# Seven block products in place of eight in nine of 22 tile pairs of an MLP, and its output product in three groups of rows

## The chip, the cores and the metric

The kernel runs on one core of a Trainium2 chip. The metric is the device time of one execution in microseconds (us). The engines are called PE (TensorE, the matmuls; PEld is its weight loads), DVE (VectorE), ACT (ScalarE), POOL (GpSimd) and SP (SyncE, which issues the DMAs). Each engine takes its instructions from a queue of its own, in order.

## The reference

A network on 16 + 512 positions of 1024 features: a layer with differential attention, a layer with latent attention, and a mixer with a convolution and sliding attention. Each ends in a gated MLP of the same kind with 2816 = 22 x 128 hidden features, and the change is in these three MLPs alone:

```python
xn = rms_norm(h, g_norm)
a, b = jnp.split(xn @ w_in, 2, axis=-1)
ap = jnp.pad(a, ((0, 0), (CONV_W - 1, 0), (0, 0)))
a_conv = conv_b
for j in range(CONV_W):
    a_conv = a_conv + ap[:, j:j + L] * conv_w[j]
return h + (jax.nn.silu(a_conv) * b) @ w_out
```

The first MLP has 528 positions, the second 514 on the a side and 512 on the b side, the third 512.

## The kernel before

Features lie on partitions, positions along the free axis. h, the residual stream, stays in SBUF in float32. Each heavy product keeps the precision of float32 with reduced-precision operands: a tensor is split into a high part (a cast) and a low part (the rest), and `lin` (L243) issues three matmuls for each tile of 128 input features: high x high, high x low, low x high. All of them are line 254.

Weights come through the class `Weights` (L73) by one plan, a list of chunks of 8 x 128 rows in the order of use. `load` issues the DMA (L86, 512 KB) three chunks ahead, `_split` makes the parts two chunks ahead: ACT casts the high part (L103), and DVE takes the low part in two halves of 512 columns (L112), or, for every fourth chunk, POOL in four pieces of 256 (L108).

`ffn` (L411) is an MLP. For each of the 22 tiles f of 128 hidden features it makes two products over all 1024 input features, a (`pa`) and b (`pb`). a is multiplied by the norm's factor R on DVE (L434, `am`); the gate follows: the first tap of the convolution on ACT (L437), two more on DVE (L441), silu on ACT (L444), times R (L445), times b (L448); and the result is split into Gh and Gl (L351, L352). R comes late: its sum of squares ends after the last residual add, so the first tile's matmuls run before R is there, and its `am` waits. In the first MLP both products run in two ranges of columns (a in 272 and 258, b in 272 and 256), in the second a in 258 and 256 and b in one of 512, in the third each in one of 512. Once all 22 tiles of G stand, `proj_h` (L398), or `finish` (L1252) in the last MLP, makes the output product: for each of 8 tiles m of output features, 22 tiles of G in three chunks of weights into one accumulation in PSUM, which is then added into h.

The order on each engine is set by a scheduler that works from the order of the code, and waits between engines are semaphores.

## Time and profile before

| | |
|---|---|
| median of 3 runs | 2115.77 us (2115.68 to 2116.41) |
| the profiled execution | 2117.24 us, of which the span of its instructions is 2115.5 |
| PE busy | 2083.4 us, 98% of the span |
| PEld busy | 1868.7 us, 88% |
| DVE busy | 1163.7 us, 55% |
| ACT busy | 858.1 us, 41% |
| POOL busy | 447.4 us, 21% |
| granted TensorE clock | 0.994 of full speed |

A busy share is an average over the span. An engine is busy while one of its instructions runs. Matmuls are pipelined, so the duration of one is longer than the distance from its start to the next one's; a rate of PE is read from starts.

### The profile page before, as it was taken

The numbers are of one execution on the slowest core, as the hardware profiler recorded it, in microseconds if no ns is written. First come the engines' busy times: TensorE is split into PE (matmuls) and PEld (weight loads), VectorE is DVE, ScalarE is ACT, GpSimd is POOL, SyncE is SP. The second block draws the span as 40 slices with busy tenths as digits, with TensorE's granted clock in tenths as the row PEclk, the third lists the DMA queues.
The fourth block names the chain that finished last, engine by engine and source line by source line (L and its number), as shares of the span: only waits on it lengthen the run. The fifth ranks groups of instructions, "written<-read, shape, count | busy, mean of one in ns | idle before, by whom it ended". The sixth has DMA issues, their size and how long they took to land.

```text
span 2115.5 us, 33036 instructions
## 1 busy us (share of the span) xinstructions
PE 2083.4 (98%) x13226; PEld 1868.7 (88%) x13226; DVE 1163.7 (55%) x2212; ACT 858.1 (41%) x1658; POOL 447.4 (21%) x555
## 2 busy tenths in 40 slices
PE   8999999999999999999999999999999999999998
PEld 8999899999999988899999888788888888888887
DVE  8687756666533477755555532675534355555322
ACT  6566544444323455543333332354422334333221
POOL 5223231111121231122111123221112231111121
PEclk9999999999999999999999999999999999999999
DMA  4111022222322211122322333222223232333331
GB/s 168 51 60 60 32 81 100 81 90 90 93 83 88 77 36 35 41 70 81 100 91 91 94 90 105 85 90 71 75 75 100 91 98 90 100 100 96 88 98 58
DMA packets 52954, 174.72 MB, mean 83 GB/s; under 512 B 6080, under 2 KB 9024, under 8 KB 52800
## 3 DMA queue, kind: packets, MB, share of 16 engines
q1 hardware_dynamic: 52368, 172.34, 25.7%
q8 instruction: 104, 1.70, 0.3%
q14 instruction: 50, 0.41, 0.1%
q10 hardware_dynamic: 432, 0.27, 0.1%
HBM read 170.45 MB, written 2.10 MB: 82 GB/s over the span
## 4 chain that ended last, share of the span: by engine, by line
PE 92%; DVE 5%; ACT 2%; issue 1%; POOL 0%; DMA 0%; POOLq 0%; DVEq 0%; ACTq 0%
PE po L254 24%; PE pa L254 18%; PE pb L254 18%; PE pc L254 6%; PE pq L254 5%; PE pg L254 4%; PE s L482 2%; PE pyc L254 2%; PE pd L254 2%; PE pm L254 2%; PE ph L254 1%; PE o L1122 1%; PE pya L254 1%; PE pt L1100 1%; DVE wlo L112 1%
## 5 line engine op out<-in xcount | busy, mean ns | idle before, releaser
L103 ACT CAST whi<-raw 128x1024 fp32r<-128x1024 f32 (+3 forms) x328 | 330.8, 1009 | 723.9 <-PE po L254 233.1
L108 POOL TENSOR_TENSOR wlo<-raw,whi 128x256 fp32r<-128x256 f32 (+1 forms) x342 | 264.3, 803 | 1089.8 <-ACT whi L103 1085.1
L112 DVE TENSOR_TENSOR wlo<-raw,whi 128x512 fp32r<-128x512 f32 (+2 forms) x474 | 318.7, 714 | 220.7 <-ACT whi L103 218.8
L254 PE MATMUL pa<-Xh,wlo 128*128 128x258 f32 (+3 forms) x880 | 269.3, 306 | 0.0
L254 PE MATMUL pa<-Xl,whi 128*128 128x258 f32 (+3 forms) x880 | 269.0, 306 | 0.0
L254 PE MATMUL pa<-Xh,whi 128*128 128x258 f32 (+3 forms) x880 | 268.3, 305 | 0.0
L254 PE MATMUL po<-Gl,whi 128*128 128x512 f32 (+2 forms) x726 | 244.1, 336 | 0.0
L254 PE MATMUL po<-Gh,whi 128*128 128x512 f32 (+2 forms) x726 | 242.8, 334 | 0.0
L254 PE MATMUL po<-Gh,wlo 128*128 128x512 f32 (+2 forms) x726 | 242.5, 334 | 0.0
L254 PE MATMUL pb<-Xh,wlo 128*128 128x512 f32 (+2 forms) x704 | 238.9, 339 | 0.0
L254 PE MATMUL pb<-Xl,whi 128*128 128x512 f32 (+2 forms) x704 | 238.7, 339 | 0.0
L254 PE MATMUL pb<-Xh,whi 128*128 128x512 f32 (+2 forms) x704 | 238.1, 338 | 0.0
L254 PEld LDWEIGHTS pa<-Xl,whi 128*128 128x128 f32 x880 | 165.6, 188 | 8.6
L254 PEld LDWEIGHTS pa<-Xh,whi 128*128 128x128 f32 x880 | 165.8, 188 | 8.2
L254 PEld LDWEIGHTS pa<-Xh,wlo 128*128 128x128 f32 x880 | 166.1, 189 | 6.6
L254 PEld LDWEIGHTS po<-Gh,whi 128*128 128x128 f32 x726 | 136.6, 188 | 16.2
L254 PEld LDWEIGHTS po<-Gh,wlo 128*128 128x128 f32 x726 | 136.4, 188 | 14.8
L254 PEld LDWEIGHTS po<-Gl,whi 128*128 128x128 f32 x726 | 136.7, 188 | 14.3
L254 PEld LDWEIGHTS pb<-Xh,wlo 128*128 128x128 f32 x704 | 132.6, 188 | 14.5
L254 PEld LDWEIGHTS pb<-Xh,whi 128*128 128x128 f32 x704 | 132.4, 188 | 14.2
L254 PEld LDWEIGHTS pb<-Xl,whi 128*128 128x128 f32 x704 | 132.4, 188 | 14.1
L434 DVE TENSOR_TENSOR am<-pa,R 128x272 f32<-128x272 f32 (+2 forms) x110 | 52.9, 481 | 141.9 <-PE pa L254 133.8
(394 smaller groups left out, 4468.9 us busy)
## 6 DMA issues: line engine op xcount, KB each, us to landing
raw<-in_w_in_dram SPq DMA_DIRECT2D x134, 512.0 KB, 3.4
raw<-in_w_up_dram SPq DMA_DIRECT2D x44, 512.0 KB, 3.4
raw<-in_w_out_dram SPq DMA_DIRECT2D x32, 512.0 KB, 3.5
raw<-in_w_qkv_dram SPq DMA_DIRECT2D x24, 512.0 KB, 3.5
raw<-in_w_o_dram SPq DMA_DIRECT2D x16, 512.0 KB, 3.4
raw<-in_w_dn_dram SPq DMA_DIRECT2D x16, 512.0 KB, 3.5
raw<-in_w_out_dram SPq DMA_DIRECT2D x16, 384.0 KB, 3.1
raw<-in_w_co_dram SPq DMA_DIRECT2D x8, 512.0 KB, 3.4
```

The lines of the kernel that those rows point to most:

```text
L103: nc.scalar.copy(h, r)
L108: nc.gpsimd.tensor_tensor(l[:, c], r[:, c], h[:, c].bitcast(F32), op=ALU.subtract)
L112: nc.vector.tensor_tensor(l[:, c], r[:, c], h[:, c].bitcast(F32), op=ALU.subtract)
L254: nc.tensor.matmul(ps, w, x, start=first and i == 0, stop=last and i == len(ops) - 1)
L434: nc.vector.tensor_tensor(am[:, sa - a0 : ea - a0], pa[:, : ea - sa], R[:, sa:ea], op=ALU.mult)
L482: nc.tensor.matmul(s[:, :w], qa[:, q0 : q0 + P], ka[:, k0:k1], start=z == 0, stop=z == len(ops) - 1 and not masked,)
L1100: nc.tensor.transpose(t[:, b * P : (b + 1) * P], p[:, j, a : a + P], self.ident)
L1122: nc.tensor.matmul(o[:, i, j, :], st[n, "pt", j][:, b * P : (b + 1) * P], V[:, b, c], start=n % 4 == j == b == 0, stop=False,)
```

## The change

The 22 tiles are put in three groups (`GROUPS`): 8, 7 and 7 tiles. Nine times two tiles (f, g) form a pair; tiles 0, 1, 14 and 21 stay plain. In a pair, g is done as before. The tile f takes its a rows and b rows together: a and b are two rows of blocks, the input features two columns (the tiles 0 to 3 and 4 to 7), the positions two halves, and a product of 2 x 2 by 2 x 2 blocks that takes 8 block products is done by 7, with sums of weights and of inputs. A block product is 12 matmuls (four tiles of features, three matmuls each) on half of the positions: 264 columns in the first MLP, 258 in the second, 256 in the third.

The sums of inputs, four for each of four tiles of features, are T0 to T3. `differences` makes them once in each MLP, after tile 0 in the code: for each k, ACT scales h into x, DVE forms four tensors in one buffer d, ACT casts all four at once into Th, DVE takes the low part Tl. The sums of weights are made by POOL for each pair: S (two sums, in four pieces of 256 columns), t (two sums, four pieces) and the low part of d (two pieces). S and the d of `differences` have the same tag, "rawS", with one buffer. A pair loads two rows at once, the second into a buffer "rawA" of its own kind. The number of bytes loaded stays.

Within a pair PE's order is written out by hand. With X for the input and the weights in front: A (a rows, X), C (S, T0), half of g's a product, A += (S, T1), B (a rows, X), the rest of g's a product, A += (t, T2), half of g's b product, C += (t, X), A += (d, T3), the rest of g's b product. Between these, ACT copies A to p1, C to bm, A to u2 and A to bm, and DVE adds the pieces into `an` and `bm`. The gate works on all positions at once. Where the third MLP has one range, g's a product stands whole between C and A += (S, T1).

After each of the first two groups its output product, over 8 or 7 tiles of G, is added into h; the last group's goes on as the whole did before. In the first MLP the ranges are 264 and 264.

```diff
+GROUPS = (
+    (0, 8, (0, 1, (2, 3), (4, 5), (6, 7))),
+    (8, 15, ((8, 9), (10, 11), (12, 13), 14)),
+    (15, 22, ((15, 16), (17, 18), (19, 20), 21)),
+)
...
+    def sums(self, d, a, b, op):
+        for c in (slice(0, 256), slice(256, 512)):
+            self.net.nc.gpsimd.tensor_tensor(d[:, c], a[:, c], b[:, c], op=op)
...
+        if kind == "s":
+            self.S = self.more.tile([P, 1056], F32, tag="rawS", name=f"rawS{n}", bufs=1)
+            self.sums(self.S[:, lo], a2[:, lo], a2[:, hi], ALU.add)
+            self.sums(self.S[:, hi], self.S[:, lo], a1[:, lo], ALU.subtract)
+            return self.S[:, :1024]
+        if kind == "t":
+            self.sums(a1[:, lo], a1[:, lo], a2[:, lo], ALU.subtract)
+            self.sums(a1[:, hi], a1[:, hi], self.S[:, hi], ALU.subtract)
+            return a1
+        return a2[:, hi]
...
+                f, g = st
+                rows = [self.chunk(wi, m)[1][0] for m in (f, NF + f)]
+                pl += [((wi, f, "a"), rows, 8, P, "a"), ((wi, f, "s"), [], 8, P, "s"), self.chunk(wi, g)]
+                pl += [((wi, f, "t"), [], 8, P, "t"), self.chunk(wi, NF + g), ((wi, f, "d"), [], 4, P, "d")]
+            pl += [self.chunk(wo, m, k0, k1) for m in range(KD)]
...
+    def group_h(self, psp, name, G, k0, nk, ranges, done):
+        for m in range(KD):
+            w = [(self.W.get((name, m, k0)), 0)]
+            ps = [psp.tile([P, 512], F32, tag="mm", name=self.n("po")) for _ in ranges]
+            for a, b in ((0, nk),) if m else ((0, nk - 2), (nk - 2, nk)):
+                for p, (s, e) in zip(ps, ranges):
+                    self.lin(p[:, : e - s], w, G, s, e, part=(a, b), first=a == 0, last=b == nk)
+            for p, (s, e) in zip(ps, ranges):
+                done(p[:, : e - s], m, s, e)
...
+            def differences():
+                for k in range(4):
+                    g = self.pc(xg, k + 4)
+                    x = tp.tile([P, NT], F32, tag="am", name=self.n("x"))
+                    nc.scalar.activation(x[:, : NT - s0], self.h[:, k, s0:], AF.Identity, scale=self.pc(xg, k))
+                    x1, x2 = x[:, :H], x[:, s1 - s0 : e1 - s0]
+                    d = tp.tile([P, 1056], F32, tag="rawS", name=self.n("d"), bufs=1)
+                    d = d[:, : 4 * H].rearrange("p (t c) -> p t c", t=4)
+                    nc.vector.tensor_tensor(d[:, 0], x2, x1, op=ALU.subtract)
+                    nc.vector.scalar_tensor_tensor(
+                        d[:, 2], self.h[:, k + 4, s1:e1], g, x2, op0=ALU.mult, op1=ALU.subtract
+                    )
+                    nc.vector.tensor_tensor(d[:, 1], d[:, 2], x1, op=ALU.add)
+                    nc.vector.scalar_tensor_tensor(
+                        d[:, 3], self.h[:, k + 4, s0:e0], g, d[:, 1], op0=ALU.mult, op1=ALU.subtract
+                    )
+                    hi, lo = (t[:, :, k, :] for t in T)
+                    nc.scalar.copy(hi, d)
+                    nc.vector.tensor_tensor(lo, d, hi.bitcast(F32), op=ALU.subtract)
...
+            def pair(f, kf, g, kg):
+                get = self.W.get
+                A, B, C = bank(True), None, bank()
+                wa = get((wi, f, "a"))
+                block(A, wa, 0, (0, 0))
+                p1 = tp.tile([P, H], F32, tag="p1", name=self.n("p1"), bufs=1)
+                nc.scalar.copy(p1, A[:, :H])
+                ws = get((wi, f, "s"))
+                block(C, ws, 0, 0)
+                bm = tp.tile([P, NT], F32, tag="bm", name=self.n("bm"), bufs=1)
+                sl, hi = slice(e0 - s1, H), slice(e0 - a0, NT - a0)
+                nc.scalar.copy(bm[:, hi], C[:, sl])
+                am = tp.tile([P, NT], F32, tag="am", name=self.n("am"))
+                w = [(get((wi, g, 0)), 0)]
+                half_a(w, am, *a_ranges[0])
+                block(A, ws, 4, 1, False)
+                u2 = tp.tile([P, H], F32, tag="u2", name=self.n("u2"), bufs=1)
+                nc.scalar.copy(u2, A[:, :H])
+                B = bank()
+                block(B, wa, 4, (1, 0))
+                an = tp.tile([P, NT], F32, tag="am", name=self.n("am"))
+                nc.vector.tensor_tensor(an[:, :H], p1, B[:, :H], op=ALU.add)
+                for s, e in a_ranges[1:]:
+                    half_a(w, am, s, e)
+                t = gate(g, am)
+                wt = get((wi, f, "t"))
+                block(A, wt, 0, 2, False)
+                nc.vector.tensor_tensor(bm[:, hi], A[:, sl], bm[:, hi], op=ALU.add)
+                w = [(get((wi, NF + g, 0)), 0)]
+                half_b(w, t, *b_ranges[0])
+                block(C, wt, 4, (1, 1), False)
+                nc.vector.tensor_tensor(an[:, hi], u2[:, sl], C[:, sl], op=ALU.add)
+                block(A, get((wi, f, "d")), 0, 3, False)
+                nc.scalar.copy(bm[:, :H], A[:, :H])
+                for s, e in b_ranges[1:]:
+                    half_b(w, t, s, e)
+                self.split(*G.at(kg, t0, NT), t)
+                nc.vector.tensor_tensor(an[:, : NT - a0], an[:, : NT - a0], R[:, a0:], op=ALU.mult)
+                t = gate(f, an)
+                nc.vector.tensor_tensor(t, bm[:, o : o + n], t, op=ALU.mult)
+                self.split(*G.at(kf, t0, NT), t)
...
+            for k0, k1, steps in GROUPS:
+                for i, st in enumerate(steps):
+                    if isinstance(st, int):
+                        plain(st, st - k0)
+                    else:
+                        with self.in_order():
+                            pair(st[0], st[0] - k0, st[1], st[1] - k0)
+                    if k0 == i == 0:
+                        differences()
+                if k1 < NF:
+                    self.group_h(psp, wo, G, k0, k1 - k0, ranges, add)
...
-        self.ffn("w_in0", "w_out0", "cw0", "cb0", ((0, 272), (270, NT)), HALVES, functools.partial(self.open_x, None))
+        even = ((0, 264), (264, NT))
+        nxt = functools.partial(self.open_x, None)
+        self.ffn("w_in0", "w_out0", "cw0", "cb0", even, even, even, HALVES, nxt)
```

In the orders below, numbers in names tell instances apart: weights 36 are the a rows of tile 2 (and, after the change, with a second row 36_1, its b rows), 37 is the next chunk: before it is tile 2's b rows, after it is S. pf is a bank of a product, the first number behind Th or Xh that of the buffer.

**DVE, first MLP, at the end of tile 1.** Before, steps of the gates of tiles 0 and 1, and the low part of weights 37 among them:

```order
L441 SCALAR_TENSOR_TENSOR ct_616_4121<-am_614_4094,par_76,ct_616_4121 128x256 [waits Activation_49]
L441 SCALAR_TENSOR_TENSOR ct_620_4196<-am_618_4169,par_76,ct_620_4196 128x271 [waits Activation_49]
L441 SCALAR_TENSOR_TENSOR ct_616_4121<-am_614_4094,par_76,ct_616_4121 128x256 [waits DVE_49]
L441 SCALAR_TENSOR_TENSOR ct_620_4196<-am_618_4169,par_76,ct_620_4196 128x270 [waits DVE_49]
L112 TENSOR_TENSOR wlo37_4165<-raw37_4155,whi37_4164 128x512 [waits DMAHW6_49,PE_49,Activation_49]
L112 TENSOR_TENSOR wlo37_4165<-raw37_4155,whi37_4164 128x512
L445 TENSOR_TENSOR ct_616_4121<-ct_616_4121,R_604_4003 128x256 [waits Activation_49]
L445 TENSOR_TENSOR ct_620_4196<-ct_620_4196,R_604_4003 128x272 [waits Activation_49]
```

After, at the same place, the last of the four rounds of differences (k = 3), then the low part of S:

```order
L499 TENSOR_TENSOR d_625_4179<-x_624_4177 128x264 [waits DVE_49]
L500 SCALAR_TENSOR_TENSOR d_625_4179<-h_73,par_76,x_624_4177 128x264
L531 SCALAR_TENSOR_TENSOR ct_629_4244<-am_626_4191,par_76,ct_629_4244 128x526 [waits DVE_49]
L503 TENSOR_TENSOR d_625_4179<-d_625_4179,x_624_4177 128x264 [waits DVE_49]
L504 SCALAR_TENSOR_TENSOR d_625_4179<-h_73,par_76,d_625_4179 128x264 [waits DVE_49]
L535 TENSOR_TENSOR ct_629_4244<-ct_629_4244,R_604_4003 128x528 [waits Activation_49]
L549 TENSOR_TENSOR ct_629_4244<-pf_630_4262,ct_629_4244 128x264 [waits DVE_49,PE_49]
L549 TENSOR_TENSOR ct_629_4244<-pf_631_4288,ct_629_4244 128x264 [waits PE_49]
L509 TENSOR_TENSOR Tl_611_4018<-d_625_4179,Th_610_4017 128x4x264 [waits Activation_49]
L400 TENSOR_TENSOR Gl_609_4016<-ct_629_4244,Gh_608_4015 128x528 [waits Activation_49]
L154 TENSOR_TENSOR wlo37_4256<-rawS37_4250,whi37_4255 128x512 [waits Activation_49]
L154 TENSOR_TENSOR wlo37_4256<-rawS37_4250,whi37_4255 128x512 [waits Pool_49]
```

The rounds of differences stand between the steps of the gates of tiles 0 and 1; all four stand behind the first product with R (`am`, row L544), and the low part of weights 37 comes after the last Tl.

**POOL, first MLP, from tile 1 on.** Before, low parts of every fourth chunk:

```order
L108 TENSOR_TENSOR wlo35_4027<-raw35_4017,whi35_4026 128x256 [waits DMAHW4_49,PE_49,Activation_49]
L108 TENSOR_TENSOR wlo35_4027<-raw35_4017,whi35_4026 128x256 x3
L303 TENSOR_TENSOR nr_605_4004<-nv_603_4001,mhalf_99 128x5 [waits DVE_49]
L108 TENSOR_TENSOR wlo39_4301<-raw39_4291,whi39_4300 128x256 [waits DMAHW0_49,PE_49,Activation_49]
L108 TENSOR_TENSOR wlo39_4301<-raw39_4291,whi39_4300 128x256 x3
L108 TENSOR_TENSOR wlo43_4575<-raw43_4565,whi43_4574 128x256 [waits DMAHW4_49,PE_49,Activation_49]
L108 TENSOR_TENSOR wlo43_4575<-raw43_4565,whi43_4574 128x256 x3
```

After, the four pieces of S, whose first waits for DVE, then the four of t and the two of d's low part:

```order
L151 TENSOR_TENSOR wlo35_4086<-raw35_0_4024,whi35_4085 128x256 [waits DMAHW4_49,PE_49,Activation_49]
L151 TENSOR_TENSOR wlo35_4086<-raw35_0_4024,whi35_4085 128x256 x3
L351 TENSOR_TENSOR nr_605_4004<-nv_603_4001,mhalf_99 128x5 [waits DVE_49]
L110 TENSOR_TENSOR rawS37_4250<-raw36_1_4094 128x256 [waits DMAHW7_49,DVE_49]
L110 TENSOR_TENSOR rawS37_4250<-raw36_1_4094 128x256
L110 TENSOR_TENSOR rawS37_4250<-rawS37_4250,raw36_0_4092 128x256 [waits DMAHW5_49,Pool_49]
L110 TENSOR_TENSOR rawS37_4250<-rawS37_4250,raw36_0_4092 128x256 [waits Pool_49]
L110 TENSOR_TENSOR raw36_0_4092<-raw36_0_4092,raw36_1_4094 128x256 [waits DMAHW3_49,DMAHW2_49,DMAHW6_49,DMAHW1_49,Pool_49]
L110 TENSOR_TENSOR raw36_0_4092<-raw36_0_4092,rawS37_4250 128x256
L110 TENSOR_TENSOR raw36_0_4092<-raw36_0_4092,raw36_1_4094 128x256 [waits Pool_49]
L110 TENSOR_TENSOR raw36_0_4092<-raw36_0_4092,rawS37_4250 128x256
L151 TENSOR_TENSOR wlo41_4458<-raw36_1_4094,whi41_4457 128x256 [waits PE_49,Activation_49]
L151 TENSOR_TENSOR wlo41_4458<-raw36_1_4094,whi41_4457 128x256
```

In place of one low part in four pieces stand ten pieces for a pair; the buffer rawS37 is the one in which the d of the differences stood, so the first piece waits for the last Tl.

**PE, first MLP, from tile 1 to tile 2.** Before, the last matmul of tile 1's b and the first of tile 2's a:

```order
L254 MATMUL pb_625_4263<-Xh_573_3573,wlo35_4027 128x256
L254 MATMUL pa_627_4308<-Xh_573_3573,whi36_4157 128x272 [waits Activation_49]
L254 MATMUL pa_627_4308<-Xl_574_3574,whi36_4157 128x272
L254 MATMUL pa_627_4308<-Xh_573_3573,wlo36_4158 128x272 [waits DVE_49]
L254 MATMUL pa_627_4308<-Xh_573_3573,whi36_4157 128x272
```

After, the last matmuls of block A and the first of block C:

```order
L522 MATMUL pf_632_4318<-Xl_574_3574,whi36_4186 128x264
L522 MATMUL pf_632_4318<-Xh_573_3573,wlo36_4187 128x264
L522 MATMUL pf_633_4319<-Th_610_4017,whi37_4255 128x264 [waits Activation_49]
L522 MATMUL pf_633_4319<-Tl_611_4018,whi37_4255 128x264 [waits DVE_49]
L522 MATMUL pf_633_4319<-Th_610_4017,wlo37_4256 128x264 [waits DVE_49]
```

Where the next matmuls waited for weights from ACT and DVE alone, C waits for the cast of S (ACT), for Tl and for the low part of S (DVE).

## Rows read from the trace of the kernel before

**Rows 1.** Busy time (x instructions) summed over three stretches, one per MLP with work after.
```profile
sum 1284.00, PE 1274.22 PEld 1144.65 DVE 640.72 ACT 458.42 POOL 241.24; mean PE 424.74 PEld 381.55 DVE 213.57 ACT 152.81 POOL 80.41
```

**Rows 2.** PE in order of time, first MLP: start us, duration us, instruction, count.
```profile
500.40 0.28 PE L254 MATMUL pa<-Xh,whi 128*128 128x258 f32 x1
...
506.12 0.29 PE L254 MATMUL pa<-Xh,whi 128*128 128x272 f32 x1
...
512.17 0.28 PE L254 MATMUL pa<-Xh,whi 128*128 128x258 f32 x1
```

**Rows 3.** The same, second MLP.
```profile
1101.23 0.28 PE L254 MATMUL pa<-Xh,whi 128*128 128x258 f32 x1
...
1106.97 0.39 PE L254 MATMUL pb<-Xh,whi 128*128 128x512 f32 x1
...
1112.54 0.28 PE L254 MATMUL pa<-Xh,whi 128*128 128x258 f32 x1
```

**Rows 4.** The same, third MLP.
```profile
1880.80 0.39 PE L254 MATMUL pa<-Xh,whi 128*128 128x512 f32 x1
...
1891.79 0.39 PE L254 MATMUL pa<-Xh,whi 128*128 128x512 f32 x1
```

**Rows 5.** In order of time, start of each MLP (idle before it and releaser in brackets).
```profile
303.81 0.28 PE L254 MATMUL pa<-Xh,whi 128*128 128x272 f32 x1
...
312.74 0.44 DVE L434 TENSOR_TENSOR am<-pa,R 128x272 f32<-128x272 f32 x1 [3.92 <-ACT R L323]
...
329.52 0.29 PE L254 MATMUL pa<-Xh,whi 128*128 128x272 f32 x1
...
952.03 0.28 PE L254 MATMUL pa<-Xh,whi 128*128 128x258 f32 x1
...
963.84 0.42 DVE L434 TENSOR_TENSOR am<-pa,R 128x258 f32<-128x258 f32 x1
...
976.86 0.28 PE L254 MATMUL pa<-Xh,whi 128*128 128x258 f32 x1
...
1736.15 0.39 PE L254 MATMUL pa<-Xh,whi 128*128 128x512 f32 x1
...
1749.77 0.69 DVE L434 TENSOR_TENSOR am<-pa,R 128x512 f32<-128x512 f32 x1 [2.58 <-ACT R L323]
...
1759.94 0.39 PE L254 MATMUL pa<-Xh,whi 128*128 128x512 f32 x1
```

**Rows 6.** Groups by line and shape, first and third MLP: busy us, mean ns; idle before.
```profile
L112 DVE TENSOR_TENSOR wlo<-raw,whi 128x512 fp32r<-128x512 f32 x64 | 41.4, 689 | 17.8 <-ACT whi L103 17.8
...
L441 DVE SCALAR_TENSOR_TENSOR ct<-am,par,ct 128x256 f32<-128x256 f32 x44 | 21.2, 482 | 0.7
...
L445 DVE TENSOR_TENSOR ct<-ct,R 128x256 f32<-128x256 f32 x22 | 12.9, 587 | 11.7 <-ACT ct L444 11.7
...
L448 DVE TENSOR_TENSOR ct<-pb,ct 128x256 f32<-128x256 f32 x22 | 9.3, 425 | 1.5
...
L103 ACT CAST whi<-raw 128x1024 fp32r<-128x1024 f32 x42 | 44.2, 1053 | 54.0 <-PE pa L254 24.5 <-issue 15.2 <-PE pb L254 14.3
...
L441 DVE SCALAR_TENSOR_TENSOR ct<-am,par,ct 128x510 f32<-128x510 f32 x22 | 16.5, 750 | 0.7
...
L448 DVE TENSOR_TENSOR ct<-pb,ct 128x512 f32<-128x512 f32 x22 | 15.2, 692 | 9.6 <-PE pb L254 9.5
...
L437 ACT ACTIVATE ct<-am,par 128x512 f32<-128x512 f32 x21 | 17.1, 817 | 0.5 <-DVE am L434 0.4
```

**Rows 7.** In order of time, POOL and DVE, first MLP.
```profile
542.70 3.20 POOL L108 TENSOR_TENSOR wlo<-raw,whi 128x256 fp32r<-128x256 f32 x4 [20.35 <-ACT whi L103]
...
542.97 0.76 DVE L445 TENSOR_TENSOR ct<-ct,R 128x256 f32<-128x256 f32 x1 [0.99 <-ACT ct L444]
```

**Rows 8.** Near the program's start: one matmul, then the stretch with busy times, granted clock.
```profile
14.93 0.47 PE L254 MATMUL pq<-Xh,wlo 128*128 128x272 f32 x1 [0.41 <-DVE wlo L112]
...
14.90:18.40 3.50, 3.47 (x16) 3.47 (x17) 3.50 (x7) 3.50 (x12) 3.26 (x4) 0.53 0.66 235
```

More of the change, by code (lines that the diff above doesn't have):

```diff
@@ L122, in get @@
         end = len(self.plan)
+        sa = min(self.sa, self.sa if sa is None else sa)
+        while self.ns < min(n + 1 + sa, end):
+            if self.nl == self.ns:
+                self.load()
+            self._split()
         while self.nl < min(n + 1 + self.la, end):
             self.load()
-        while self.ns < min(n + 1 + min(self.sa, self.sa if sa is None else sa), end):
-            self._split()
         self.nu += 1
@@ L253, in lin @@
         for i, (w, x) in enumerate(ops):
-            nc.tensor.matmul(ps, w, x, start=first and i == 0, stop=last and i == len(ops) - 1)
+            nc.tensor.matmul(ps, w, x, start=first and i == 0, stop=i == len(ops) - 1, skip_group_check=not first)
             if hooks and i in hooks:
@@ new lines, in block @@
+            def block(ps, w, c, x, first=True):
+                ops = []
+                for k in range(4):
+                    if isinstance(x, int):
+                        xh, xl = (t[:, x, k, :] for t in T)
+                    else:
+                        xh, xl = X.at(4 * x[0] + k, *quads[x[1]])
+                    hi, lo = w[0][:, c + k, :], w[1][:, c + k, :]
+                    ops += [(hi, xh), (hi, xl), (lo, xh)]
+                for i, (a, b) in enumerate(ops):
+                    nc.tensor.matmul(ps[:, :H], a, b, start=first and i == 0, stop=i == len(ops) - 1, skip_group_check=not first)
@@ new lines, in gate @@
+            def gate(f, am):
+                w0, w1, w2 = (self.pc(cw, j * NF + f) for j in range(3))
+                t = tp.tile([P, NT], F32, tag="ct", name=self.n("ct"), bufs=3)[:, :n]
+                nc.scalar.activation(t, am[:, o : o + n], AF.Identity, scale=w2, bias=self.pc(cb, f))
+                for d, w in ((1, w1), (2, w0)):
+                    z = 0 if o >= d else d
+                    a = o + z - d
+                    nc.vector.scalar_tensor_tensor(
+                        t[:, z:], am[:, a : a + n - z], w, t[:, z:], op0=ALU.mult, op1=ALU.add
+                    )
+                nc.scalar.activation(t, t, AF.Silu)
+                nc.vector.tensor_tensor(t, t, R[:, t0:], op=ALU.mult)
+                return t
@@ new lines, in bank, with half_a, half_b @@
+            def bank(first=False):
+                return (self.psg if first else psp).tile([P, 512], F32, tag="mm", name=self.n("pf"))
+            def half_a(w, am, s, e, first=False):
+                ps = bank(first)
+                self.lin(ps[:, : e - s], w, X, s, e)
+                nc.vector.tensor_tensor(am[:, s - a0 : e - a0], ps[:, : e - s], R[:, s:e], op=ALU.mult)
+            def half_b(w, t, s, e, first=False):
+                ps = bank(first)
+                self.lin(ps[:, : e - s], w, X, s, e)
+                nc.vector.tensor_tensor(t[:, s - t0 : e - t0], ps[:, : e - s], t[:, s - t0 : e - t0], op=ALU.mult)
@@ new lines, in plain @@
+            def plain(f, k):
+                w = [(self.W.get((wi, f, 0)), 0)]
+                am = tp.tile([P, NT], F32, tag="am", name=self.n("am"))
+                for z, (s, e) in enumerate(a_ranges):
+                    half_a(w, am, s, e, f == 0 and z == 0)
+                t = gate(f, am)
+                w = [(self.W.get((wi, NF + f, 0)), 0)]
+                for z, (s, e) in enumerate(b_ranges):
+                    half_b(w, t, s, e, f == 0 and z == 0)
+                self.split(*G.at(k, t0, NT), t)
```

130 lines of the change are left out of this document (62 added, 68 removed).

## The prediction

> **What bounds the kernel now.** Read first the three stretches that hold the MLPs [rows 1]: of 1284.0 us PE is busy 1274.2, DVE 640.7 and POOL 241.2. TensorE hardly waits, so the change gains only by matmuls that it takes away, and it loses whatever it makes TensorE wait. Then read PE in order of time, from one start to the next, since the durations of matmuls overlap. In the first MLP 48 matmuls of 256 and 258 columns go from 500.40 to 506.12 (0.119 us each) and 48 of 272 columns on to 512.17 (0.126): a tile takes 11.77 [rows 2]. In the second, 48 of 258 and 256 columns take 5.74 (0.1196), 24 of 512 columns 5.57, a tile 11.31 [rows 3]. In the third a tile is 48 matmuls of 512 columns, 10.99 [rows 4].
>
> **What goes.** In a pair the first tile is done by 7 blocks of 12 matmuls, each on half of the columns: 84. The first MLP has 264 columns a half, between its two rows: 0.122, so 10.25 in place of 11.77, 1.52 less. The second: 84 x 0.1196 = 10.05 for 11.31, 1.26 less. The third has no row with half the columns; with 0.119 from rows 2 it is 10.00 for 10.99, 0.99 less. Nine pairs in each give 13.7 + 11.3 + 8.9 = 33.9, and even halves of 264 give the 13 other tiles of the first MLP 96 x 0.122 = 11.73, 0.04 less each, 0.5. The sum is **-34.4 us**. It is the surest term: the row of each is the same instruction on the same operands' shapes.
>
> **What the first pair of each MLP waits for.** The second block of a pair, C, takes the sum of weights S and the differences T0. By the order of DVE's queue all four rounds of differences stand in it among the gates of tiles 0 and 1, and all of them behind the first product with R, since that queue is in order. S lies in the one buffer that the differences d use too, so POOL may form the first S only after the last Tl has been read out of it; ACT then casts it and DVE takes the low part, and only then can C start. PE's own order in a pair is fixed: everything else on PE stands behind C.
>
> When is that? Before, DVE's first product with R starts at 312.74, 963.84 and 1749.77, and PE is at the third tile at 329.52, 976.86 and 1759.94 [rows 5]. Block A is 12 matmuls, so PE would reach C at 331.0, 978.3 and 1761.4. Durations [rows 6]: 0.43 for two tensors of 256 to 264 columns, 0.49 for the form with a scalar, 0.69 and 0.75 for these at 512, 0.69 also for half of a weight's low part. A Tl of 1024 to 1056 has no row; from 0.425 at 256 and 0.692 at 512, which is 0.267 for each 256, I estimate 1.23 to 1.26.
> - First MLP: 16 x 0.43 + 8 x 0.49 + 4 x 0.69 + 4 x 0.77 + 3 x 0.72 + 4 x 1.26 = 23.8, so the last Tl ends at 336.6 at the earliest. POOL's four sums take 3.20 [rows 7], ACT's cast 1.05 [rows 6], and 0.45 of the low part is not covered: 341.3. PE is idle 10.3.
> - Second: 12 x 0.43 + 8 x 0.49 + 2 x 0.69 + 4 x 0.75 + 5 x 0.69 + 4 x 1.24 = 21.9, so 985.7, and S at 990.4: idle 12.1.
> - Third: 8 x 0.43 + 8 x 0.49 + 4 x 0.75 + 7 x 0.69 + 4 x 1.23 = 20.1, so 1769.9, and S at 1774.6: idle 13.2.
>
> These 35.6 us suppose that DVE never waits. It takes some 14 things from ACT in each of these stretches (x and Th four times, ct, silu and Gh of two gates). Where DVE waits for a silu now it idles 11.7 us in 22 times, 0.53 each [rows 6]; if none of the 14 is covered, that is 7.4 an MLP, if all are, nothing. The queue alternates gate and difference, so I take a third, 2.5 an MLP: **+43** (35.6 to 58).
>
> **The clock after such a wait.** After an idle 0.41 us the matmuls of 272 columns ran at a granted clock of 0.53, 16 of them in 3.47 us [rows 8], where 0.126 each would be 2.0; the lower of the two levels, 1.2 GHz, for that stretch. Three such starts are **+4.5**; a longer wait is not in the trace, so I keep 0 to 9.
>
> **The other 24 pairs.** A pair takes PE 22.0, 21.4 and 21.0 us in the three MLPs (10.25 + 11.73, and so on). DVE has in it, at 512 columns, ten halves of low parts (6.9), two gates (4 x 0.75 + 2 x 0.69), half_a, half_b and two products with R or bm (2.8), three adds of blocks (1.3) and two Gl (1.4): 16.8. POOL has 10 operations of 0.80, 8.0. The two meet: while POOL's four ran from 542.70, a product on DVE that takes 0.425 elsewhere took 0.76 [rows 7], 0.34 more. With 0.34 for each of the ten, DVE has 20.2 in 21.0: it just keeps up. The Trainium skill says in "SBUF — State Buffer", section "Who interferes with whom", that a VectorE instruction with two SBUF inputs and a GpSimd instruction that reads SBUF exclude each other, the later one blocked until the first is done. The 0.34 of the row would be the rest of one POOL operation, which agrees; by the rule's worst case, 0.80 for each, the DVE sum is 24.8 and the term below is the one of the second rival. So near to full, single deliveries will come late: I take **+3** for it over all pairs (0 to 10).
>
> In the third MLP there is less room. A += (wt, T2) overwrites the bank that ACT copies to u2, and it follows the block before by one block only (1.43 us), because that MLP has one a range, where the others have half of g's columns in between. In ACT's queue u2 stands behind the Gh of the pair before, the cast of d and g's ct. Counted from the end of g's half_a: DVE's product 0.69, ct 0.82 [rows 6], u2 about half of that, 1.9 in all, against two blocks of PE, 2.85, if DVE and ACT are free. If part of the earlier pair's gate (4.4 us of DVE steps) still stands ahead it is late, by up to 2. Six such passages at 1: **+6** (0 to 12).
>
> **At the ends.** The weights' traffic stays the same; the sums need a second row of weights in SBUF at a time, and the load is issued 3 ahead as before. At the end of each group the gate of the last f is covered by 55 to 66 matmuls of the output product that don't read its rows (8 us and more against 4.4 us of DVE steps); if that cover failed it would cost up to 4.4 at nine places, which I hold for unlikely and leave in the upper end. The added adds into h, two groups of 8 or 16 on DVE, lie beside the output product. The last product has 7 rows in place of 22 to cover the work at the very end: **+1** (0 to 3).
>
> **How the numbers follow.** -34.4 + 43 + 4.5 + 3 + 6 + 1 = +23.1 on the profiled execution of 2117.2, so 2140.3. The median of the runs is 1.5 lower: **2139**. All low ends give -34.4 + 35.6 = +1.2, so 2117; high ends that come together in part, +52, 2168. About 0.2% (4.2 us, 2111.5 to 2120.0) is what a measurement of this kernel can tell from no change. Cases:
> - The forecast, idle at the first pairs of 10 to 17 us each, more than the gain: 2121 to 2160, **0.72**.
> - Rival one, faster: the first S is not late. DVE is idle 3.92 us before its first product with R [rows 5] and half its time on average [rows 1], so if the differences stood early or the last Tl were done by the time of C, only small terms are left: 2117.2 - 34.4 + 3 + 6 + 1 - 1.5 = 2091. It decides at (34.4 - 10) / 3 = 8 us of idle with the clock in it: below that per MLP the change gains. Against it stands that DVE's bound alone gives 10 to 13. **0.09**.
> - Rival two, slower still: DVE sets the pace of pairs. If each of POOL's 10 operations holds DVE for its whole 0.80, a pair is 24.8 long and not 21.0 to 22.0: 2.8 to 3.8 in each of 24 pairs, on average 3.3, is +80; on 2139 it is 2219, and half of that 2179. The point from which it decides is 0.42 per operation in the third MLP (4.2 free of 21.0); the row has 0.34. The Trainium skill's rule of rival exclusion, named above, is what would bring it. **0.09**.
> - Rival three, no change: the first pairs lose only their lower bounds and nothing else is late, 2117 to 2120, or the two cancel below that. **0.10**.
>
> Faster is so 0.09, same 0.10, slower 0.81. The range 2117 to 2168 leaves out the first rival, most of the second and part of the third, about 0.2.
>
> **What would show it.** In the profile after, each MLP has one idle of PE of 10 to 17 us, about 27, 26 and 25 us after its first matmul, ended by ACT's cast of a weight (the line of the weights' cast), and ahead of it POOL's four sums start right after a Tl on DVE. Behind it about 3.5 us of matmuls at half the clock. PE busy falls by about 34 less what the slow clock adds. The pairs after that run at 21 to 22 us. I am wrong if that idle is below 8 us (then DVE's sum or its place in the queue was misread), or if idle is spread over all pairs (then rival two holds).

## The result and the profile after

The changed kernel takes 2129.95 us (median of 4 runs, 2128.76 to 2132.29) where the kernel before took 2116.09 (2115.68 to 2116.89). The ratio is 1.0066, 95% interval 1.0049 to 1.0084: 14 us slower. The prediction was 2139, with 2117 to 2168 as its range. The profiled execution has 2129.86 us, its span 2128.0. In the runs below two executions were slow and are left out of every figure: one of ten of the first experiment (6656 us) and one of the kernel before beside it (5487 us).

From the page of the kernel after: the span; busy time of each engine; the chain that ended last, by engine; and, of the costliest groups, block products on the differences, with the idle time of PE ahead of them at the row's end.

```profile
span 2128.0 us, 34085 instructions
...
PE 2054.2 (97%) x13505; PEld 1861.4 (87%) x13505; DVE 1335.5 (63%) x2410; ACT 935.7 (44%) x1778; POOL 600.2 (28%) x723
...
PE 79%; DVE 9%; issue 5%; ACT 4%; POOL 2%; DMA 2%; SPq 0%; ACTq 0%; POOLq 0%; DVEq 0%
...
L522 PE MATMUL pf<-Th,whi 128*128 128x264 f32 (+2 forms) x432 | 124.9, 289 | 41.4 <-ACT whi L147 38.2
```

PE is busy 29 us less than before (2054.2 against 2083.4), and DVE 172 us more, POOL 153 more. Before, the chain that ended last was, by engine:

```profile
PE 92%; DVE 5%; ACT 2%; issue 1%; POOL 0%; DMA 0%; POOLq 0%; DVEq 0%; ACTq 0%
```

PE's share has fallen from 92% to 79%: there are stretches now in which PE waits for others. Which, the waits of PE say (who waited for whom: us in total, times, longest):

```profile
PE pf L522 <- ACT whi L147: 38.2, 3, 14.3
...
PE pf L522 <- ACT u L580: 3.2, 3, 1.9
```

Before, no product of an MLP had such a wait. All 38.2 us of the first row are three waits, one in each MLP. The chain of the first of them, in order of time (start, duration, engine, line, instruction; in brackets the idle time before and what ended it): the first product with R and the last Tl on DVE, the four sums on POOL, the cast on ACT, and block C.

```profile
310.12 0.43 DVE L544 TENSOR_TENSOR am<-pf,R 128x264 f32<-128x264 f32 x1 [3.72 <-ACT R L371]
...
334.39 1.25 DVE L509 TENSOR_TENSOR Tl<-d,Th 128x1056 fp32r<-128x1056 f32 x1
...
335.72 1.80 POOL L110 TENSOR_TENSOR rawS<-raw 128x256 f32<-128x256 f32 x2 [28.07 <-DVE Tl L509]
...
337.48 1.40 POOL L110 TENSOR_TENSOR rawS<-rawS,raw 128x256 f32<-128x256 f32 x2
...
338.92 1.04 ACT L147 CAST whi<-rawS 128x1024 fp32r<-128x1024 f32 x1 [3.77 <-POOL rawS L110]
...
340.01 0.59 PE L522 MATMUL pf<-Th,whi 128*128 128x264 f32 x1 [11.45 <-ACT whi L147]
```

The reader is to see a relay: Tl ends at 335.64, POOL starts at 335.72; POOL ends at 338.88, ACT starts at 338.92; ACT ends at 339.96, PE starts at 340.01. In the other two MLPs it is the same, DVE's first product with R, its last Tl, and C:

```profile
959.65 0.42 DVE L544 TENSOR_TENSOR am<-pf,R 128x258 f32<-128x258 f32 x1
...
981.13 1.23 DVE L509 TENSOR_TENSOR Tl<-d,Th 128x1032 fp32r<-128x1032 f32 x1
...
986.71 0.58 PE L522 MATMUL pf<-Th,whi 128*128 128x258 f32 x1 [12.44 <-ACT whi L147]
...
1750.25 0.68 DVE L544 TENSOR_TENSOR am<-pf,R 128x512 f32<-128x512 f32 x1
...
1770.13 1.22 DVE L509 TENSOR_TENSOR Tl<-d,Th 128x1024 fp32r<-128x1024 f32 x1
...
1775.70 0.58 PE L522 MATMUL pf<-Th,whi 128*128 128x256 f32 x1 [14.30 <-ACT whi L147]
```

What stands behind each of these waits on PE, in stretches (the columns: window, width, busy us of PE, PEld, DVE, ACT and POOL with their instructions, then the granted clock, the DMA share and GB/s):

```profile
340.00:343.70 3.70, 3.65 (x15) 3.35 (x16) 2.00 (x3) 1.14 (x2) 2.53 (x3) 0.50 0.00 0
...
986.70:992.00 5.30, 5.25 (x22) 4.95 (x23) 3.60 (x5) 2.27 (x3) 2.52 (x3) 0.50 0.00 0
...
1775.70:1781.00 5.30, 5.25 (x18) 4.52 (x19) 3.60 (x5) 2.26 (x3) 2.52 (x3) 0.51 0.00 0
```

For 3.7, 5.3 and 5.3 us the clock was 0.50 to 0.51, the lower level of 1.2 GHz; PE had been idle 11.5 to 14.3 us before it.

A count by PE's starts, from the first matmul of one part to the first of the next, puts the whole difference in its place. The part "at the end" is in the output products.

| us | to the first MLP | three MLPs, input products | output products and end | between MLPs | span |
|---|---|---|---|---|---|
| before | 303.8 | 755.7 | 388.0 | 668.0 | 2115.5 |
| after | 301.4 | 771.1 | 387.3 | 668.2 | 2128.0 |

So the input products, which have 324 fewer matmuls on half of the positions (12 for each of 27 pairs), take 15.4 us longer, the output product in three groups costs nothing, and 2.4 us are won ahead of the first MLP, where the change does nothing (more on that at the end).

### The profile page after: what moved, and what is told of

Read it like the earlier page. It is cut to its first block, busy times and chain, and to the rows that moved or that the text cites. A ratio compares the mean times of both kernels' runs of the same rounds, so it can differ in the third digit from the quotient of the medians.

```text
span 2128.0 us, 34085 instructions
## 1 busy us (share of the span) xinstructions
PE 2054.2 (97%) x13505; PEld 1861.4 (87%) x13505; DVE 1335.5 (63%) x2410; ACT 935.7 (44%) x1778; POOL 600.2 (28%) x723
## 4 chain that ended last, share of the span: by engine, by line
PE 79%; DVE 9%; issue 5%; ACT 4%; POOL 2%; DMA 2%; SPq 0%; ACTq 0%; POOLq 0%; DVEq 0%
PE po L302 24%; PE pf L302 16%; PE pf L522 10%; PE pc L302 6%; PE pg L302 4%; PE pq L302 3%; DVE wlo L154 2%; PE pyc L302 2%; PE s L651 2%; PE pm L302 2%; PE pd L302 2%; ACT whi L147 1%; PE ph L302 1%; PE o L1291 1%; DMA raw<-in_w_up_dram 1%
## 5 line engine op out<-in xcount | busy, mean ns | idle before, releaser
L302 PE MATMUL pf<-Xh,whi 128*128 128x264 f32 (+3 forms) x936 | 301.3, 322 | 0.0
L302 PE MATMUL pf<-Xl,whi 128*128 128x264 f32 (+3 forms) x936 | 300.7, 321 | 0.0
L302 PE MATMUL pf<-Xh,wlo 128*128 128x264 f32 (+3 forms) x936 | 300.2, 321 | 0.0
L302 PEld LDWEIGHTS pf<-Xh,wlo 128*128 128x128 f32 x936 | 177.6, 190 | 13.3
L302 PEld LDWEIGHTS pf<-Xh,whi 128*128 128x128 f32 x936 | 177.6, 190 | 12.1
L302 PEld LDWEIGHTS pf<-Xl,whi 128*128 128x128 f32 x936 | 177.5, 190 | 11.4
L522 PE MATMUL pf<-Th,whi 128*128 128x264 f32 (+2 forms) x432 | 124.9, 289 | 41.4 <-ACT whi L147 38.2
L522 PE MATMUL pf<-Th,wlo 128*128 128x264 f32 (+2 forms) x432 | 124.4, 288 | 0.1
L522 PE MATMUL pf<-Tl,whi 128*128 128x264 f32 (+2 forms) x432 | 123.8, 287 | 0.0
L302 PE MATMUL pq<-Xh,whi 128*128 128x272 f32 (+1 forms) x384 | 114.5, 298 | 1.4 <-ACT whi L147 1.4
```

What stands on the lines that cost most here:

```text
L302: nc.tensor.matmul(ps, w, x, start=first and i == 0, stop=i == len(ops) - 1, skip_group_check=not first)
L522: nc.tensor.matmul(ps[:, :H], a, b, start=first and i == 0, stop=i == len(ops) - 1, skip_group_check=not first)
```

## The experiments

The theory: the change's own gain is there as counted, some 34 us; the loss is the wait at the first pair of each MLP, with the slow clock behind it; and that wait is DVE's queue of differences and gates after R, then POOL, ACT and the shared buffer in a row. The rivals: the gain is smaller than counted; or pairs run at the pace of DVE and POOL, and the wait is only where that shows first. Each run stands beside runs of the kernel before on the same chip, whose medians were 2114.5 to 2115.8.

**A buffer of its own for the differences.**

```diff
-                    d = tp.tile([P, 1056], F32, tag="rawS", name=self.n("d"), bufs=1)
+                    d = tp.tile([P, 1056], F32, tag="dd", name=self.n("d"), bufs=1)
...
-                t = tp.tile([P, NT], F32, tag="ct", name=self.n("ct"), bufs=3)[:, :n]
+                t = tp.tile([P, NT], F32, tag="ct", name=self.n("ct"), bufs=2)[:, :n]
```

> The d of the differences gets a buffer of its own, so that POOL's first S no longer waits for the last Tl (to make room, S's buffer is 1024 wide and the gate's buffer ct has two copies in place of three). Theory (the idle before the first C is DVE's queue plus, behind it, POOL's four sums 3.2 us, ACT's cast 1.05 and DVE's low part, because the buffer is shared): S is ready early, and C waits for the last Tl alone. In the first MLP that ends at about 335.6, with 2.6 us of low parts moved ahead of it up to 338, where C's matmuls of k = 3 would run at 329.5: idle 6 to 8.7 us in place of 11.5, and the same in the other two; 3 to 5.5 us less in each, 2114 to 2121. Rival (the sums themselves, POOL and the buffer, are the last thing, not DVE): the idle falls below 2 us in each and the time to about 2092.

2119.4 us (nine runs), ratio 1.0022 (1.0013 to 1.0032). Waits of PE:

```profile
PE pf L522 <- ACT Th L508: 16.8, 7, 3.6
...
PE pf L522 <- DVE Tl L509: 6.6, 7, 1.6
```

C no longer waits for S at all; in its place PE waits for Th and Tl themselves, 23.4 us in all against 38.2. Taking POOL, ACT and the low part out of the relay (4.35 us each time) gives some 10 us, within the theory's 2114 to 2121, and not the 38 of the rival: DVE's queue is the long part of the wait, the shared buffer the short one.

**The differences ahead of tile 0.**

```diff
                 for i, st in enumerate(steps):
+                    if k0 == i == 0:
+                        differences()
...
-                    if k0 == i == 0:
-                        differences()
```

> The differences stand ahead of tile 0 in the code, so that the first two rounds of the four stand ahead of the first product with R in DVE's queue. Theory (DVE's queue sets the time at which S is free, and DVE is idle 5.5 to 6 us ahead of that product): the idle at the first C falls by 4 to 6 us in each MLP, to 6 to 9, and the time to 2112 to 2118. Rival (what counts is the number of hand-offs between ACT and DVE after R, or R itself comes later because DVE's and ACT's steps for it now stand behind the rounds): less than 2 us is gained in each, 2124 to 2130 or more.

2108.9 us, ratio 0.9968 (0.9956 to 0.9981). Waits of PE:

```profile
PE pf L522 <- ACT whi L147: 12.1, 3, 6.4
```

The three waits for S go from 38.2 to 12.1 (2.1, 3.6 and 6.4). The theory expected 18 to 27 to be left; it was right in kind and too careful in size. DVE now does the first two rounds while R is on its way, at a price: R itself comes later, and PE waits 2.5 us for it in the first MLP. The kernel beats the one before by 6 us.

**Four plain tiles first.** The same nine pairs, in groups of 8, 8 and 6.

```diff
-    (0, 8, (0, 1, (2, 3), (4, 5), (6, 7))),
-    (8, 15, ((8, 9), (10, 11), (12, 13), 14)),
-    (15, 22, ((15, 16), (17, 18), (19, 20), 21)),
+    (0, 8, (0, 1, 2, 3, (4, 5), (6, 7))),
+    (8, 16, ((8, 9), (10, 11), (12, 13), (14, 15))),
+    (16, 22, ((16, 17), (18, 19), (20, 21))),
```

> Still nine pairs in each MLP, but the groups are 8, 8 and 6 tiles, and four plain tiles (0 to 3) stand ahead of the first pair in place of two. Theory (the three idle times of 38.2 us and the slow clock behind them, about 7, are all that the change lost; the blocks saved are worth 33 to 34): DVE has two more tiles of PE time, 22 to 23.5 us, for the same work, so the first C waits for nothing; 2130 - 38 - 7 = 2085, with the waits for u2 left (3). Rival (DVE and POOL are so loaded that the backlog only moves to later pairs, or the saved blocks are worth less): idle of PE appears in later pairs, time above 2105.

2086.64 us, ratio 0.9867 (0.9852 to 0.9882); the forecast of the theory was 2085. It ran again later as the base of other runs:

> Four plain tiles ahead of the first pair and groups of 8, 8 and 6, once more, as the base of the other three runs: 2086.6 within 2 us, no idle of PE at the first pairs.

2085.72 us, ratio 0.9863 (0.9850 to 0.9877). The input products take 723.7 and 724.2 us, 47 less than in the changed kernel and 32 less than before. So the idle time was not a sign of something else: with two more tiles of PE time ahead of the first pair it is gone and does not come back later. Of the 47 us, 38.2 are the waits. The rest, 9, is the slow clock: 7.2 by half of the three stretches above, and 1.7 by half of a fourth, which stands in the changed kernel behind its longest wait for u2 (1.85 us, the PE row at 1940.84 further on):

```profile
1941.30:1944.70 3.40, 3.40 (x15) 3.11 (x14) 3.34 (x7) 1.06 (x2) 1.50 (x2) 0.50 0.34 103
```

The kernel with four plain tiles waits about as long for u2 in all (2.5 and 3.8 us in its two traces), but no stretch of its input products is at the lower level.

**All tiles plain, in three groups.** This computes the same and has neither pairs nor differences.

```diff
-    (0, 8, (0, 1, (2, 3), (4, 5), (6, 7))),
+    (0, 8, tuple(range(0, 8))),
...
-                    if k0 == i == 0:
-                        differences()
```

> The 22 tiles all plain, with the output product in three groups and the even ranges as in the changed kernel; no pairs, no differences. Theory (the groups cost nothing, since the adds into h lie beside matmuls, and the even ranges give 1 us): 2116 as before, within 3 us; the 2.4 us by which the first MLP starts earlier in the changed kernel stay or go, as the scheduler has it. Rival (the three groups cost something at each boundary that the comparison of the traces hides in the pairs): 2122 or more.

2111.2 us, ratio 0.9984 (0.9974 to 0.9993), 3.5 us faster than before. The rival is out: the groups cost nothing. The input products take 753.1 against 755.7, all of the 2.5 in the first MLP, where a tile with even halves takes 11.65 (81.58 us for seven) and not the 11.73 interpolated in the prediction; the output products 386.7 against 388.0.

**The late copy u2.** In the third MLP, g's b product goes ahead of A += (t, T2), on the base with four plain tiles.

```diff
+                if not late:
+                    half_b(w, t, *b_ranges[0])
                 block(A, wt, 0, 2, False)
                 nc.vector.tensor_tensor(bm[:, hi], A[:, sl], bm[:, hi], op=ALU.add)
+                if late:
+                    half_b(w, t, *b_ranges[0])
```

> On the base with four plain tiles, in the third MLP alone, g's b product (24 matmuls, 5.5 us) moves ahead of A += (t, T2), so that ACT's copy u2 has that much longer. Theory (PE's waits in the third MLP come from u2, which stands in ACT's queue behind the gate of the pair before): the four waits for u2, 2.5 us in all, go, and the time falls by 2 to 3 us against the base. Rival (the gate of the pair before is the late one, and another step of it, the copy to bm or the cast of S, is late next, now that the end of the pair has nothing behind it): the waits move to another block, and the time stays within 1 us of the base or rises.

2085.5 us, ratio 0.9853 (0.9839 to 0.9866): by the medians no difference from the base, 0.2 us. In the trace all waits for u2 are gone, and the third MLP, from its first matmul to the end of the span, takes 369.9 us where the base has 373.3 and 373.7. So the theory's gain is in the trace, 3.5 us, and not in the medians; two profiled runs of the base differ by as much ahead of the first MLP alone (the last section).

**How much room has DVE?** Added work on DVE in each pair: the low part of G of tile f formed 4 times more, then 12 times more.

```diff
                 self.split(*G.at(kf, t0, NT), t)
+                for _ in range(4):
+                    nc.vector.tensor_tensor(gl, t, gh.bitcast(F32), op=ALU.subtract)
```

> On the base with four plain tiles each pair has four more operations on DVE (the low part of G of tile f again, 0.7 us each, 2.8 in all), which change nothing in the result. Theory (DVE needs 14.5 to 15.7 us of a pair's 21 to 22, so 5 to 6 are free): no new wait of PE beyond the delays of single deliveries, 2087 to 2093. Rival (DVE and POOL hold each other up so much that pairs already run at DVE's pace, the second rival of the prediction): 2.8 us for each of 27 pairs, 2150 or more.

2104.7 us (two runs), ratio 0.9949 (0.9931 to 0.9967): 19 us slower than the base, where the theory allowed 7. The base first: busy times of the group of four pairs in the first MLP, in the second and in the third (columns as above).

```profile
440.70:528.00 87.30, 87.30 (x723) 87.30 (x722) 62.75 (x101) 40.43 (x60) 29.38 (x34) 1.00 0.30 92
...
1069.50:1155.10 85.60, 85.60 (x626) 81.38 (x625) 59.84 (x93) 39.68 (x59) 31.71 (x37) 1.00 0.31 93
...
1844.60:1929.40 84.80, 83.72 (x529) 75.42 (x528) 58.39 (x89) 39.40 (x59) 29.55 (x37) 1.00 0.30 94
```

DVE has 62.8, 59.8 and 58.4 us in four pairs, 15.7, 15.0 and 14.6 each: 6.1 to 6.6 us free in a pair of 21.2 to 21.8. With 2.8 more there should be room. In the loaded kernel the third MLP's group has

```profile
1856.00:1944.50 88.50, 84.43 (x530) 75.60 (x530) 66.83 (x101) 39.13 (x59) 35.22 (x37) 1.00 0.29 90
```

and PE's waits are

```profile
PE pf L522 <- ACT u L580: 7.7, 4, 2.5
...
PE pc L302 <- DVE Xl L403: 5.0, 2, 3.4
...
PE pf L302 <- DVE wlo L154: 3.0, 6, 1.2
```

DVE is far from full, 66.8 of 88.5, and still PE waits. The POOL column of the third MLP's rows shows one way: its 37 pieces take 35.2 us in place of 29.6. Ahead of the longest wait for u2 (2.5 us) no added operation stands directly before the late gate, but two pieces of POOL on the low part of d, which take 1.43 in the base (the first row), take 2.33 beside two added operations, and the first two of the next S take 2.39 where the base has 1.44:

```profile
1875.82 1.43 POOL L151 TENSOR_TENSOR wlo<-raw,whi 128x256 fp32r<-128x256 f32 x2 [10.30 <-ACT whi L147]
...
1887.28 2.33 POOL L151 TENSOR_TENSOR wlo<-raw,whi 128x256 fp32r<-128x256 f32 x2 [10.30 <-ACT whi L147]
...
1888.93 1.23 DVE L606 TENSOR_TENSOR Gl<-ct,Gh 128x512 fp32r<-128x512 f32 x1
...
1893.39 2.39 POOL L110 TENSOR_TENSOR rawS<-raw 128x256 f32<-128x256 f32 x2 [3.78 <-DMA raw<-in_w_up_dram]
```

The load between the two lands 3.8 us after d's pieces in both kernels, so S comes 1.8 us later, and with it what follows in the pair. The last Xl for the mixer is late in another way: four added operations stand ahead of a stretch of 32 us in which DVE shows no idle time (1284.7 to 1317). The other waits were not followed. So the rival is refuted in size (2150) and right in kind, since the two engines do hold each other up; and the theory is refuted: free time on average is not slack for a delivery.

> The same with twelve more operations in each pair, 8.4 us. Theory: DVE then needs 23 to 24 us in a pair of 21 to 22 and sets the pace, 1.5 to 2.2 us late per pair, less what the output products between groups give back: 2105 to 2140, with PE waiting in every MLP. Rival (DVE waits for other engines in such a way that the added work falls into its idle time): below 2100.

2197.95 us (two runs), ratio 1.0390 (1.0371 to 1.0409), beyond both. PE's waits:

```profile
PE po L302 <- DVE Gl L606: 56.3, 15, 6.3
...
PE pf L302 <- DVE wlo L154: 10.8, 9, 1.8
```

The larger part is not the pace of pairs but the added operations of each group's last pair: they write the G that the output product reads next, and PE waits for them up to 6.3 us at a time. In the pairs themselves the theory's size holds where it can be read: in the first MLP the group of four takes 94.2 us in place of 87.3, 1.7 more a pair (1.5 to 2.2 expected), with DVE busy for 79.8 of it, not full. What the theory left out is what a late last gate costs at a group's end; as a measure of DVE's capacity the run's total is inconclusive.

**The last group of 8.** The base's wait behind the second MLP, from its waits of PE (in the first row the u2 of the third MLP):

```profile
PE pf L522 <- ACT u L580: 3.8, 3, 1.7
...
PE pc L302 <- DVE Xl L403: 2.5, 1, 2.5
```

In the changed kernel, with 7 tiles in the last group, that row is not there. The stretch from the second MLP to the third is 409.6 us there, 410.0 before, 409.7 to 411.3 in the other three kernels with a last group of 7, and 412.3 to 413.8 with a last group of 6. So the groups again in another order, 8, 6 and 8, with the u2 edit kept:

```diff
-    (8, 16, ((8, 9), (10, 11), (12, 13), (14, 15))),
-    (16, 22, ((16, 17), (18, 19), (20, 21))),
+    (8, 14, ((8, 9), (10, 11), (12, 13))),
+    (14, 22, ((14, 15), (16, 17), (18, 19), (20, 21))),
```

> Four plain tiles first, g's b product ahead of A += (t, T2) in the third MLP, and the groups of 8, 6 and 8 tiles in place of 8, 8 and 6. Theory (with a last group of 6 tiles the output product of the second MLP leaves 4.2 us a row of h, too little for the adds, squares and splits of the next norm, so that the mixer's first product waits 2.55 us for the last Xl and starts again at the low clock; with 8 tiles it is 5.6 us a row): that wait goes, the stretch from the second MLP to the third falls from 413 to about 409.5 us, and the time to 2079 to 2083. Rival (the mixer's longer stretch comes from another order of its own instructions): the stretch stays at 412 to 414 and the time at 2085.

2079.52 us, ratio 0.9832 (0.9819 to 0.9846), 35 us faster than the kernel before and 50 faster than the change. The stretch is 409.95. From its page and its waits of PE, the longest wait and the only one of a `pc`:

```profile
span 2078.9 us, 34095 instructions
...
PE 2045.9 (98%) x13508; PEld 1855.6 (89%) x13508; DVE 1348.3 (65%) x2412; ACT 937.7 (45%) x1778; POOL 603.8 (29%) x713
...
PE s L655 <- ACT qk L822: 5.0, 2, 2.5
...
PE pc L302 <- ACT whi L147: 0.9, 1, 0.9
```

No product of an MLP waits for more than 0.14 us: the kernel is where it was before the change, bound by PE, with fewer matmuls. By the table's parts it has 303.0, 730.6, 376.7 and 668.6 us; since in the third MLP parts of pairs now run among the output products, the middle two are to be read together: 1107.3 against 1143.7 before, 36.4 less.

## Why the prediction was right, and where its terms were off

The mechanism was named in advance with its place, and the trace shows it in that place; the time came out 9 us better than forecast because the losses were taken too high, less one that was taken too low, and because of 2.4 us ahead of the first MLP which no term holds (the last section). In the traces the terms, in the order of the sum, measure -35.0 (32.5 and 2.5, below) + 38.2 + 8.9 + 0 + 3.2 - 0.7, and -2.2 outside the MLPs: 12.4, where the spans differ by 12.5 and the sum had 23.1.

- **The gain, -34.4.** Right. The kernel with all tiles plain and the last one, which has the pairs, another order of groups and no long wait in an MLP, differ by 1139.8 - 1107.3 = 32.5 us in input and output products, where nine pairs in each MLP were put at 33.9. The even halves, put at 0.04 a tile, gave 0.11 (2.5 us in 22 plain tiles); the groups gave 1.3 in the output products.
- **The first pair, +43.** 38.2. The three parts of the wait, forecast and measured:

| us | 1st MLP | 2nd | 3rd |
|---|---|---|---|
| DVE, first product with R to last Tl: sum / measured | 23.8 / 25.5 | 21.9 / 22.7 | 20.1 / 21.1 |
| POOL, ACT and what else to C: sum / measured | 4.7 / 4.4 | 4.7 / 4.4 | 4.7 / 4.4 |
| DVE's first product to PE's arrival at C: sum / measured | 18.3 / 18.4 | 14.5 / 14.6 | 11.6 / 11.2 |
| idle of PE: lower bound / measured | 10.3 / 11.5 | 12.1 / 12.4 | 13.2 / 14.3 |

  That the sums come so near is in part luck, two errors against each other. These are the stretches of the table's first row (columns as above):

```profile
310.12:335.64 25.52, 18.44 (x152) 18.23 (x151) 21.79 (x40) 14.01 (x18) 0.00 (x0) 0.96 0.07 22
959.65:982.36 22.71, 14.61 (x100) 13.36 (x99) 20.00 (x37) 12.51 (x17) 0.00 (x0) 0.92 0.07 23
1750.25:1771.35 21.10, 11.15 (x55) 9.21 (x53) 18.30 (x33) 11.79 (x16) 0.00 (x0) 0.82 0.07 25
```

  POOL does nothing in them, as forecast. DVE's instructions are the 39, 35 and 31 of the sums, and their durations add up to 23.7, 21.7 and 19.9; but the records of neighbours overlap (a d of 0.43 us starts at 310.75, the next at 311.10), so DVE is busy for only 21.8, 20.0 and 18.3. The lower bounds were thus no lower bounds, 5.7 us too high in all. Against that, DVE is idle for 3.7, 2.7 and 2.8 us, nearly all of it until ACT delivers: the 2.5 an MLP taken for the hand-offs was 1.7 us short in all, not too long. The estimate of 1.23 to 1.26 for a Tl, from [rows 6], measured 1.22 to 1.26.
- **The clock, +4.5.** Too small: 7.2 by half of the three stretches at half the clock, 8.9 with the one behind u2, which the prediction did not have; by the difference to the kernel with four plain tiles it is 9. I took the 3.5 us of [rows 8], which stand in the trace behind six waits of 0.21 to 1.07 us and not behind one of 0.41; here the clock stayed low for 3.7, 5.3 and 5.3 us. I had written that a longer wait was not in the trace and kept 0 to 9, so the range had it.
- **The other pairs, +3.** Nothing: in the first two MLPs no pair waits behind the first. Busy time in one pair of each MLP of the changed kernel:

```profile
463.00:485.00 22.00, 22.00 (x184) 22.00 (x183) 16.98 (x27) 10.27 (x16) 8.63 (x10) 1.00 0.30 96
...
1107.00:1128.00 21.00, 21.00 (x155) 19.95 (x155) 15.72 (x24) 9.19 (x13) 8.74 (x10) 1.00 0.32 99
...
1918.00:1939.00 21.00, 20.99 (x132) 18.81 (x132) 15.71 (x24) 8.60 (x13) 8.26 (x11) 1.00 0.30 98
```

  DVE has 17.0 of 22, 15.7 of 21 and 15.7 of 21, near the 16.8 of the sum at rest, and not the 20.2 with 0.34 added for each POOL operation. The two do stretch each other, which a view by shape of the group 452.9 to 530.0 shows (mean ns behind the comma):

```profile
L154 DVE TENSOR_TENSOR wlo<-rawS,whi 128x512 fp32r<-128x512 f32 x4 | 3.9, 1024 | 2.8 <-ACT whi L147 2.8
...
L400 DVE TENSOR_TENSOR Gl<-ct,Gh 128x528 fp32r<-128x528 f32 x6 | 4.4, 735 | 2.4 <-ACT Gh L399 2.4
...
L600 DVE TENSOR_TENSOR am<-am,R 128x528 f32<-128x528 f32 x3 | 3.2, 1061 | 0.0
...
L110 POOL TENSOR_TENSOR rawS<-rawS,raw 128x256 f32<-128x256 f32 x4 | 3.8, 973 | 0.0
```

  half of a low part 1024 ns where it is 689 in [rows 6], the product with R 1061 where Gl of the same width takes 735, and a POOL piece 973 where [rows 7] has 800. Against the same shapes alone, DVE's operations in this group lose 4.9 us to it, 1.6 a pair and not 3.4, and POOL's pieces lose 5.0. Only operations with both inputs in SBUF are longer, by up to 0.55 us; the nine beside POOL that read PSUM (L544, L549, L594) take 0.42 to 0.43, with POOL or without. The Trainium skill's rule of exclusion ("SBUF — State Buffer", "Who interferes with whom") agrees with these rows in kind, since none of their operations is lengthened by more than one operation of the other engine; its worst case, POOL's whole 8 us in DVE's sum, is refuted for this kernel. So what was wrong was to charge every POOL operation with the stretch of a single row. That the busy time shows none of it is again the overlap of neighbouring records: the group's durations add up to 59.6 us, its busy time is 55.0.
- **u2 in the third MLP, +6.** 3.2, at three of six places, and by the chain that was named; with the slow clock behind one of them 4.9. One of the three, DVE's last step of the earlier gate, then ACT's Gh, g's ct, u2, and PE:

```profile
1937.77 1.12 DVE L602 TENSOR_TENSOR ct<-bm,ct 128x512 f32<-128x512 f32 x1
...
1938.92 0.62 ACT L399 CAST Gh<-ct 128x512 fp32r<-128x512 f32 x1 [1.40 <-DVE ct L602]
...
1939.71 0.81 ACT L527 ACTIVATE ct<-am,par 128x512 f32<-128x512 f32 x1
...
1940.42 0.36 ACT L580 COPY u<-pf 128x256 f32<-128x256 f32 x1
...
1940.84 0.39 PE L522 MATMUL pf<-Th,whi 128*128 128x256 f32 x1 [1.85 <-ACT u L580]
```

  The product on DVE took 1.12 and not 0.7 while POOL formed the low part of d.
- **The ends, +1.** Nothing, 0.7 us less in the output products. But the same term, a last group too small to cover what follows, was real at another place when the last group became 6: I had looked for it at the program's end alone, and it came behind the second MLP.
- **The rivals.** Rival one, faster, was told apart by the idle at the first pairs: it would decide below 8 us, and measured 11.5 to 14.3. Where that idle is taken away the kernel lands on 2086, near the 2091 which that rival was given. Rival two is refuted by the pairs' PE time: four of them take 87.3, 85.6 and 84.8 us in the windows of the kernel with four plain tiles, 21.8, 21.4 and 21.2 each, where 22.0, 21.4 and 21.0 were forecast without it.

## What to carry to other kernels

Work that saves matmuls needs inputs made ready, and the first time they are needed is the place to price: count what the preparing engine's queue holds from the moment it can start to the moment PE arrives, instruction by instruction. A sum of durations came within 2 us here, because overlapping records and waits for ACT, 5.2 and 9.2 us in the three MLPs, pulled against each other; count both. The fix (two more ordinary tiles first) cost nothing in the MLPs, though the last group of 6 that came with it cost 2.5 us behind the second MLP until the groups were put in another order. A shared buffer turns such a wait into a relay over several engines, so look at tags as well as at data. And an average of free time says little: before adding an operation, look at what is due behind it in its queue, and at what another engine does beside it.
